# A decoder layer's opening in four contraction groups of four, the first begun tile by tile

## The chip, the cores and the metric

The kernel runs on one core of a Trainium2 chip. The metric is the device time of one execution in microseconds, the median of several runs. The engines are named as in the profile: PE (matrix products; PEld its weight loads), DVE (vector engine), ACT (scalar engine), POOL, and SP, whose queue issues nearly all transfers.

## The reference

One layer of a decoder, on 256 positions of width 2048, in float32. Only its beginning matters here:

```python
mod = jax.nn.silu(c) @ w_ada[l] + b_ada[l]               # c: (1, 2048), w_ada: (2048, 6 * 2048)
sh1, sc1, g1, sh2, sc2, g2 = jnp.split(mod[:, None, :], 6, axis=-1)
h = x * (1.0 + sc1) + sh1                                # x: (256, 2048)
proj = h @ w_in[l]                                       # then attention, DeltaNet, gates, LayerNorm
...
x = layer_norm(DEEPNORM_ALPHA * x + g1 * y, ln1_g[l], ln1_b[l])
h = x * (1.0 + sc2) + sh2
y = swiglu(h, w_ffn_in[l], w_ffn_out[l])
x = layer_norm(DEEPNORM_ALPHA * x + g2 * y, ln2_g[l], ln2_b[l])
```

So no product with `w_in` can start before `silu(c)` is there, columns of `w_ada` have been summed against it (shift and scale of the same rows of `h`), and x and `w_in` have been loaded.

## The kernel before

Everything is held transposed: `hTh`/`hTl` are h as 16 k tiles of 128 features x 256 positions. Every float32 operand of a product is split in two parts of the reduced type fp32r: `hi` is the value cast down (ACT, `split_w`, L221), `lo` what is missing (DVE, L222); for h that is done in `split` (L229, L230). A product of two such operands is three products: hi with the high part of h (L306), hi with its low part (L307), lo with the high part (L308), in `ws_mm`.

- **c.** `load_c` loads c into one row of `cb`, spreads it over 128 partitions by four products with a row of ones (`ps_c`, L136), and ACT writes silu of each quarter back to `cb` (L137).
- **Modulation.** `ada_opening` loads one column tile of `w_ada` after the other (1 MB each, L263) into a ring of four buffers (`r`, `ring`). `ada_sum` multiplies it by `cb` and sums, in one DVE instruction (L241), to one column of `adac`; the bias comes from `cols`. Column j is the shift of k tile j, column 16 + j its scale. `ada_to(n)` emits the sums up to the nth; `ada_goal` says how many are due at which step. The tiles of `w_ada` come in the order `ada_order`.
- **h.** `prep` forms h for some k tiles: scale plus one (`sc1p`, L442), scale and shift on ACT into `hf` (L445), then the split.
- **The opening's blocks.** `jobs` are 24 column blocks of `w_in`, 256 columns each: 16 for DeltaNet's q, k, v and 8 for attention's q, k. The contraction over 16 k tiles is cut in `GROUPS`, here 2, 3, 3, 4, 4 tiles. `startup(n)` passes over all 24 blocks for group n: load the block's k tiles of `w_in` (`raw`, `load_w`, L212), split, multiply. The first 19 blocks go to a PSUM buffer that is drained after each group: copied by ACT in the first group (L487), added by DVE to what is there in the others (L489). The last five (`KEPT`) stay in PSUM banks of their own (`mm_kept`) over all groups.
- **Order.** `step` and `do` write a program, `run(3)` starts loads and splits up to three steps ahead; the Tile layer then sets each engine's queue and the waits. A queue is served in order. The buffers are rings: six `raw`, four `hi`, four `lo`, four `r`.

Behind the opening stand `add_ba` (48 small products, L454), the two mixers, the projections and the feed-forward part, which the change does not touch.

Of the kernel before, what the change touches and what calls it, by code (L numbers as in the profile page):

```python
# [65 lines left out]
class Packed:  # L66
# [12 lines left out]

    def laid(self):  # L80
        out = np.empty(self.weight.size, np.float32)
        at = 0
        for k0, kn, c0, cn, by_column in self.tiles:
            n = P * kn * cn
# [9 lines left out]
def layer(ctx, tc, a, out):  # L94
# [32 lines left out]
    cb = perm.tile([P, D], F32, name="cb")  # L127

    def load_c():
        ones = e2("ones", [1, P])  # L130
        v_.memset(ones, 1.0)
        dma.dma_start(cb[0:1, :], a["c"])
        for i in range(4):
            ps = (pt.tile([P, 512], F32, tag="tp", name="ps_c") if i % 2 else
                  pg.tile([P, 512], F32, tag="gd", name="ps_c"))
            t_.matmul(ps, ones, cb[0:1, 512 * i:512 * i + 512], start=True, stop=True)  # L136
            s_.activation(cb[:, 512 * i:512 * i + 512], ps, AF.Silu)  # L137
# [12 lines left out]
    v_.memset(epsc[:, 0:1], RMS_EPS)  # L150
    v_.memset(epsc[:, 1:2], LN_EPS)
# [106 lines left out]
    def ada_opening(order, ahead, at_once, between):  # L258
        held, loaded = [], 0
        for n, col in enumerate(order):  # L260
            while loaded < min(at_once if n < at_once else n + ahead + 1, len(order)):
# [5 lines left out]
            ada_sum(col, 0, held.pop(0), 1)  # L267
# [9 lines left out]
    prog = []  # L277

# [95 lines left out]
    sc1p = perm.tile([P, KT], F32, name="sc1p")  # L374
# [40 lines left out]
    EARLY = 8  # L415

    def between(n):
        if n == 2 * GROUPS[0][1]:
            load_x(*GROUPS[0])

    ada1 = ada_opening(ada_order[:2 * KT + EARLY], 3, 2 * GROUPS[0][1], between)
# [7 lines left out]
    def ada_goal(n, i):  # L429
        ends = [2 * (k0 + kn) for k0, kn in GROUPS] + [2 * KT + EARLY]  # L430
        mark = 17
        if i >= mark:
            lo, hi, f = ends[min(n + 1, 5)], ends[min(n + 2, 5)], (i - mark) / len(jobs)
        else:
            lo, hi, f = ends[n], ends[n + 1], (i + len(jobs) - mark) / len(jobs) if n else (i + 1) / (mark + 1)
# [4 lines left out]
    def prep(k0, kn):  # L440
        q = slice(k0, k0 + kn)
        v_.tensor_scalar(sc1p[:, q], adac[:, 16 + k0:16 + k0 + kn], 1.0, None, op0=OP.add)  # L442
        for f in range(k0, k0 + kn):
            hf = e2("hf", [P, S])
            s_.activation(hf, x_sb[:, f, :], AF.Identity, bias=adac[:, f:f + 1], scale=sc1p[:, f:f + 1])  # L445
            split(hTh[:, f, :], hTl[:, f, :], hf)
# [10 lines left out]

    load_c()
    dma.dma_start(cols, a["cols"])
    ada_to(2 * GROUPS[0][1])  # L460
    prep(*GROUPS[0])

    KEPT = 5
    kept = []

    def startup(n):
        k0, kn = GROUPS[n]
        more = n + 1 < len(GROUPS)
        if more:
# [4 lines left out]
        for i, (c0, dst) in enumerate(jobs):  # L474
            def post(hi, lo, i=i, dst=dst):
# [4 lines left out]
                else:  # L480
                    if n == 0:
                        p, tag, b = ((pt, "tp", 2), (pt, "tp", 2), (pg, "gd", 2), (pg, "gd", 2), (pm, "mk", 1))[stays]
                        kept.append(p.tile([P, 512], F32, tag=tag, name="mm_kept", bufs=b))
                    ps = kept[stays]
                    ws_mm(ps, h_ops, hi, lo, k0, kn, n == 0, not more)
# [5 lines left out]
                if more and i == 17:  # L491
# [619 lines left out]
    jk = perm.tile([P, 40], F32, name="jk")  # L1111

# [271 lines left out]
```

## Time and profile before

| | |
|---|---|
| timed runs (us) | 1708.44, 1716.80, 1711.41; median 1711.41 |
| profiled execution, first to last instruction (us) | 1708.3 |
| mean granted TensorE clock | 0.992 |
| PE busy | 1651.7 us, 97% of the span, 11077 products |
| DVE, ACT busy | 1235.5 us (72%), 838.7 us (49%) |
| moved | 412.72 MB, mean 242 GB/s |

The page gives only the span for the profiled execution; what lies around it is not in the trace. "Idle before" in the tables is the time an engine sat idle ahead of such instructions, with the engine and line that ended most of it. A row of the timeline gives start, length, engine, line, operation, and in brackets the idle time before it and its releaser. In a row by stretches the columns are the stretch, its length, busy time of PE, PEld, DVE, ACT, POOL with counts of instructions, the granted TensorE clock, the share of the transfer engines, and GB/s.

### The profile page before, as it was taken

The numbers are of one execution on the slowest core, as the hardware profiler recorded it, in microseconds if no ns is written. First come the engines' busy times: TensorE is split into PE (matmuls) and PEld (weight loads), VectorE is DVE, ScalarE is ACT, GpSimd is POOL, SyncE is SP. The second block draws the span as 40 slices with busy tenths as digits, with TensorE's granted clock in tenths as the row PEclk, the third lists the DMA queues.
The fourth block names the chain that finished last, engine by engine and source line by source line (L and its number), as shares of the span: only waits on it lengthen the run. The fifth ranks groups of instructions, "written<-read, shape, count | busy, mean of one in ns | idle before, by whom it ended". The sixth has DMA issues, their size and how long they took to land.

```text
span 1708.3 us, 28200 instructions
## 1 busy us (share of the span) xinstructions
PE 1651.7 (97%) x11077; PEld 1482.3 (87%) x11077; DVE 1235.5 (72%) x1768; ACT 838.7 (49%) x1199; POOL 34.6 (2%) x60
## 2 busy tenths in 40 slices
PE   5899999999999998999999999999999999999997
PEld 4899999888999798889988998888888888888885
DVE  6899999787985676557989786666666666455454
ACT  3544445579653763364434454444444444433341
POOL 0000000010010000000000000000000000000000
PEclk9999999999999999999999999999999999999998
DMA  9999996666775577557899477777777776665661
GB/s 369 338 355 343 352 338 217 202 195 199 237 260 186 172 229 244 189 187 242 312 358 362 150 226 256 231 227 232 231 227 231 236 230 221 234 192 189 200 191 72
DMA packets 113750, 412.72 MB, mean 242 GB/s; under 512 B 13405, under 2 KB 14445, under 8 KB 108109
## 3 DMA queue, kind: packets, MB, share of 16 engines
q1 hardware_dynamic: 110178, 400.13, 69.4%
q0 software_dynamic: 3440, 10.80, 2.4%
q8 instruction: 87, 1.43, 0.3%
q14 instruction: 45, 0.37, 0.1%
HBM read 406.59 MB, written 4.28 MB: 241 GB/s over the span
## 4 chain that ended last, share of the span: by engine, by line
PE 61%; DVE 8%; DMA 5%; issue 2%; ACT 1%; DVEq 0%; ACTq 0%
PE mm L313 17%; PE mm L317 9%; PE mm L354 7%; PE mm L355 7%; PE mm L356 7%; DMA raw_a<-in_w_ada 4%; DVE lo L222 3%; PE mm L306 3%; PE mm L307 3%; PE mm L308 3%; DVE raw_a L241 1%; DMA Mb<-mbd 1%; PE ps L754 1%; DMA raw<-in_w_out 0%; ACT hi L221 0%
## 5 line engine op out<-in xcount | busy, mean ns | idle before, releaser
L221 ACT CAST hi<-raw 128x1024 fp32r<-128x1024 f32 (+2 forms) x576 | 582.6, 1015 | 706.2 <-PE mm L356 197.1
L222 DVE TENSOR_TENSOR lo<-raw,hi 128x1024 fp32r<-128x1024 f32 (+2 forms) x576 | 673.5, 1177 | 295.8 <-ACT hi L221 293.4
L306 PE MATMUL mm<-s,hi 128*128 128x256 f32 x1232 | 350.7, 285 | 15.9 <-ACT s L229 12.0
L308 PE MATMUL mm<-s,lo 128*128 128x256 f32 x1232 | 348.0, 283 | 13.1 <-DVE lo L222 12.9
L307 PE MATMUL mm<-s,hi 128*128 128x256 f32 x1232 | 346.8, 282 | 0.0
L313 PE MATMUL mm<-s,hi 128*128 128x512 f32 x1280 | 319.5, 392 | 0.0
L313 PEld LDWEIGHTS mm<-s,hi 128*128 128x128 f32 x1280 | 228.5, 188 | 39.4
L306 PEld LDWEIGHTS mm<-s,hi 128*128 128x128 f32 x1232 | 234.3, 190 | 21.0 <-ACT s L229 13.6
L308 PEld LDWEIGHTS mm<-s,lo 128*128 128x128 f32 x1232 | 235.8, 192 | 15.7 <-DVE lo L222 15.5
L307 PEld LDWEIGHTS mm<-s,hi 128*128 128x128 f32 x1232 | 234.8, 191 | 1.5 <-issue 1.1
L317 PEld LDWEIGHTS mm<-s,lo 128*128 128x128 f32 x1280 | 169.9, 188 | 13.6
L317 PE MATMUL mm<-s,lo 128*128 128x256 f32 x1280 | 171.9, 277 | 0.0
L354 PE MATMUL mm<-hi,ach 128*128 128x512 f32 x352 | 137.0, 389 | 0.0
L356 PE MATMUL mm<-hi,acl 128*128 128x512 f32 x352 | 136.9, 389 | 0.0
L355 PE MATMUL mm<-lo,ach 128*128 128x512 f32 x352 | 136.9, 389 | 0.0
L241 DVE CUSTOM_DVE_ANT_0 raw_a<-raw_a,cb,ada_half 128x1024 f32<-128x1024 f32 x56 | 71.7, 1280 | 53.3 <-DMA raw_a<-in_w_ada 53.3
L241 DVE CUSTOM_DVE_ANT_0 raw_a<-raw_a,cb,cols 128x1024 f32<-128x1024 f32 x56 | 71.8, 1281 | 51.1 <-DMA raw_a<-in_w_ada 51.0
L241 DVE CUSTOM_DVE_ANT_0 r<-r,cb,cols 128x2048 f32<-128x2048 f32 x40 | 93.4, 2346 | 9.4 <-ACT cb L137 9.4
L354 PE MATMUL mm<-hi,s 128*128 128x512 f32 x192 | 78.7, 410 | 0.0
L355 PEld LDWEIGHTS mm<-lo,ach 128*128 128x128 f32 x352 | 66.1, 188 | 13.8
L354 PEld LDWEIGHTS mm<-hi,ach 128*128 128x128 f32 x352 | 66.1, 188 | 13.8
L356 PEld LDWEIGHTS mm<-hi,acl 128*128 128x128 f32 x352 | 66.1, 188 | 13.6
(314 smaller groups left out, 2265.6 us busy)
## 6 DMA issues: line engine op xcount, KB each, us to landing
raw<-in_w_ffn_in SPq DMA_DIRECT2D x176, 512.0 KB, 4.3
raw<-in_w_in SPq DMA_DIRECT2D x160, 512.0 KB, 4.3
raw_a<-in_w_ada SPq DMA_DIRECT2D x112, 512.0 KB, 4.5
raw<-in_w_ffn_out SPq DMA_DIRECT2D x88, 512.0 KB, 4.2
r<-in_w_ada SPq DMA_DIRECT2D x40, 1024.0 KB, 8.0
raw<-in_w_in SPq DMA_DIRECT2D x48, 384.0 KB, 5.7
raw<-in_w_proj_gdn SPq DMA_DIRECT2D x32, 512.0 KB, 4.6
raw<-in_w_out SPq DMA_DIRECT2D x32, 512.0 KB, 5.9
```

The lines of the kernel that those rows point to most:

```text
L221: s_.copy(hi, raw)
L222: low = v_.tensor_tensor(lo, raw, hi.bitcast(F32), op=OP.subtract)
L241: v_.tensor_tensor_reduce(out=raw, in0=raw, in1=cb[:, n * part:n * part + n], scale=1.0, scalar=cols[:, col:col + 1] if first else h, op0= ...
L306: t_.matmul(o, hi[:, i, c], ah, start=(first and i == 0 and t == 0), stop=False)
L307: t_.matmul(o, hi[:, i, c], al, start=False, stop=False)
L308: t_.matmul(o, lo[:, i, c], ah, start=False, stop=(last and i == kn - 1 and t == 1))
L313: t_.matmul(box[t].rearrange("p (u i) -> p u i", u=2), hi[:, i, t * P:(t + 1) * P], both[k0 + i], start=(first and i == 0), stop=False)
L317: t_.matmul(box[t][:, :S], lo[:, i, t * P:(t + 1) * P], both[k0 + i][:, 0, :], start=False, stop=(last and i == kn - 1))
L354: t_.matmul(box[h], xh, hi[:, i, :], start=start, stop=False)
L355: t_.matmul(box[h], xh, lo[:, i, :], start=False, stop=False)
L356: t_.matmul(box[h], xl, hi[:, i, :], start=False, stop=stop)
L754: t_.matmul(ps[to, n, :], lhs(n), rhs(n), start=True, stop=True)
```

## The change

The opening has four groups of four k tiles. In the first, eight of the 24 blocks (`RAMP`: the last five, which stay in PSUM, and the first three) are begun tile by tile: for each of the k tiles 0 to 3 one x tile and two `raw` of four blocks x 256 columns of that one tile are loaded behind the tile's two columns of `w_ada`, and the products of four blocks run as soon as h of that tile is there (`ramp`). The other 16 blocks of the group follow as before, with four k tiles at once. Between the tiles of the ramp stand five products of zeros, ahead of c's products three, and behind them 22 (`warm`). The first `w_ada` column is summed in two halves. The table of ACT's functions is loaded by a small activation at the start. `prep` writes the high part of h straight from x, and a second activation the full value for the low part; the plus one of the scale goes into `cols`, once.

```diff
     def load_c():
         ones = e2("ones", [1, P])
         v_.memset(ones, 1.0)
         dma.dma_start(cb[0:1, :], a["c"])
+        ps = mm()
+        for i in range(3):
+            t_.matmul(ps, zero[:, :P], zero, start=True, stop=True)
...
     def ada_opening(order, ahead, between):
         held, loaded = [], 0
         for n, col in enumerate(order):
-            while loaded < min(at_once if n < at_once else n + ahead + 1, len(order)):
+            while loaded < min(n + ahead + 1, len(order)):
                 raw = ring[loaded % len(ring)]
                 dma.dma_start(raw, w_ada.tile(0, KT, order[loaded] * P, P, by_column=True))
                 held.append(raw)
                 loaded += 1
                 between(loaded)
-            ada_sum(col, 0, held.pop(0), 1)
+            raw = held.pop(0)
+            if n == 0:
+                for half in range(2):
+                    ada_sum(col, half, raw[:, 1024 * half:1024 * half + 1024], 2)
+            else:
+                ada_sum(col, 0, raw, 1)
             yield
...
+    def held_step(kept_raw, n, cn, post):
+        at = place["lo"]
+        prog.append((lambda: split_w(kept_raw(), n, cn, False, at), post, len(prog)))
...
-    GROUPS = [(0, 2), (2, 3), (5, 3), (8, 4), (12, 4)]
-    ada_order = [v * KT + j for k0, kn in GROUPS for j in range(k0, k0 + kn) for v in range(2)]
+    GROUPS = [(4 * n, 4) for n in range(4)]
+    ada_order = [v * KT + j for j in range(KT) for v in range(2)]
...
+    RAMP = [list(range(len(jobs) - KEPT, len(jobs) - 1)), [len(jobs) - 1, 0, 1, 2]]
+    raws = {}
 
     def between(n):
-        if n == 2 * GROUPS[0][1]:
-            load_x(*GROUPS[0])
+        if n % 2 or n > 2 * GROUPS[0][1]:
+            return
+        k = n // 2 - 1
+        load_x(k, 1)
+        for part, some in enumerate(RAMP):
+            raw = wp.tile([P, 1024], F32, tag="raw", name="raw", bufs=6)
+            dma.dma_start(raw, w_in.columns(k, [jobs[i][0] for i in some], 256))
+            raws[k, part] = raw.rearrange("p (k n) -> p k n", n=256)
...
+        if n == 0:
+            lo, hi, f = ends[0], ends[1], min((i - 2) / 14, 1)
...
     def prep(k0, kn):
-        q = slice(k0, k0 + kn)
-        v_.tensor_scalar(sc1p[:, q], adac[:, 16 + k0:16 + k0 + kn], 1.0, None, op0=OP.add)
         for f in range(k0, k0 + kn):
+            by = dict(bias=adac[:, f:f + 1], scale=adac[:, 16 + f:17 + f])
+            s_.activation(hTh[:, f, :], x_sb[:, f, :], AF.Identity, **by)
             hf = e2("hf", [P, S])
-            s_.activation(hf, x_sb[:, f, :], AF.Identity, bias=adac[:, f:f + 1], scale=sc1p[:, f:f + 1])
-            split(hTh[:, f, :], hTl[:, f, :], hf)
+            s_.activation(hf, x_sb[:, f, :], AF.Identity, **by)
+            v_.tensor_tensor(hTl[:, f, :], hf, hTh[:, f, :].bitcast(F32), op=OP.subtract)
...
+    zero = k1.tile([P, 512], F32R, tag="c2", name="zero", bufs=4)
+    v_.memset(zero.bitcast(F32), 0.0)
...
+    s_.activation(jk[:, 0:1], epsc[:, 0:1], AF.Silu)
     load_c()
     dma.dma_start(cols, a["cols"])
-    ada_to(2 * GROUPS[0][1])
-    prep(*GROUPS[0])
-
-    KEPT = 5
+    v_.tensor_scalar(cols[:, 16:32], cols[:, 16:32], 1.0, None, op0=OP.add)
+
+    def warm():
+        ps = mm()
+        two = [zero.rearrange("p (a b) -> p a b", b=b)[:, :, :b // 2] for b in (2, 32)]
+        for m in [zero] * 8 + [zero[:, 0:1].to_broadcast([P, 512])] * 3 + [zero[:, :S]] * 3 + two * 2 + [zero] * 4:
...
+            tc.keep_in_program_order(t_.matmul(o, zero[:, :P], m, start=True, stop=True))
+
+    def ramp(k, part):
+        def post(hi, lo):
+            some = RAMP[part]
...
+            for low in range(2):
+                for n, i in enumerate(some):
+                    for t in range(2):
+                        o, c = accs[i][:, t * S:(t + 1) * S], slice(t * P, (t + 1) * P)
+                        if low:
+                            last = k == 3 and t == 1 and i < len(jobs) - KEPT
+                            t_.matmul(o, lo[:, n, c], h_ops[0][k], start=False, stop=last)
+                        else:
+                            t_.matmul(o, hi[:, n, c], h_ops[0][k], start=(k == 0 and t == 0), stop=False)
+                            t_.matmul(o, hi[:, n, c], h_ops[1][k], start=False, stop=False)
+            if part and k < 3:
+                for _ in range(5):
+                    t_.matmul(kept[0], zero[:, :P], zero, start=False, stop=False)
+            if part and k == 3:
+                for i in some[1:]:
+                    s_.copy(jobs[i][1], pairs_of(accs[i]))
+
+        held_step(lambda: raws[k, part], 4, 256, post)
 
     def startup(n):
         k0, kn = GROUPS[n]
         more = n + 1 < len(GROUPS)
+        if n == 0:
+            for k in range(4):
+                do(lambda k=k: (ada_to(2 * k + 2), prep(k, 1)))
+                for part in range(2):
+                    ramp(k, part)
...
         for i, (c0, dst) in enumerate(jobs):
+            if n == 0 and i in RAMP[0] + RAMP[1]:
+                continue
```

What this makes of the queues, at three places. First SP, the issue of transfers from the program's start (`r` are columns of `w_ada`, 1 MB each; `raw` blocks of `w_in`). Before:

```order
L132 DMA cb<-in_c 1x2048
L459 DMA cols<-in_cols 128x256
L263 DMA r_95<-in_w_ada 128x2048 x2
L263 DMA r_96<-in_w_ada 128x2048
L263 DMA r_97<-in_w_ada 128x2048
L125 DMA x_sb<-in_xT 128x512
L212 DMA raw<-in_w_in 128x512 x4
L125 DMA x_sb<-in_xT 128x768
```

Now:

```order
L145 DMA cb<-in_c 1x2048
L497 DMA cols<-in_cols 128x256
L277 DMA r_93<-in_w_ada 128x2048 x2
L137 DMA x_sb<-in_xT 128x256
L449 DMA raw<-in_w_in 128x1024 x2
L277 DMA r_94<-in_w_ada 128x2048
L277 DMA r_95<-in_w_ada 128x2048
L137 DMA x_sb<-in_xT 128x256
L449 DMA raw<-in_w_in 128x1024 x2
```

The first `raw` have moved from behind four `w_ada` columns to behind two. Further on in SP's queue now, from the ramp's last tile (L449) to the blocks that are loaded as before (L226):

```order
L137 DMA x_sb<-in_xT 128x256
L449 DMA raw<-in_w_in 128x1024 x2
L277 DMA r_93<-in_w_ada 128x2048 x2
L277 DMA r_94<-in_w_ada 128x2048
L226 DMA raw<-in_w_in 128x1024 x4
L137 DMA x_sb<-in_xT 128x1024
```

Three columns of `w_ada` stand between the ramp's last `raw` and the next block's. The same place in DVE's queue now: the ramp's last `lo`, then the sums, then the `lo` of the next blocks (`s_86` is the low part of h).

```order
L236 TENSOR_TENSOR lo<-raw,hi 128x1024
L479 TENSOR_TENSOR s_86<-hf,s_85 128x256
L236 TENSOR_TENSOR lo<-raw,hi 128x1024
L255 ISA r_93,adac<-r_93,cb,cols 128x2048
L255 ISA adac 128x1
L255 ISA r_93,adac<-r_93,cb,cols 128x2048
L255 ISA adac 128x1
L255 ISA r_94,adac<-r_94,cb,cols 128x2048
L255 ISA adac 128x1
L236 TENSOR_TENSOR lo<-raw,hi 128x1024 x4
```

Three sums stand ahead of the four `lo` that the next blocks need. Last PE, from its start to the first real products; before:

```order
L136 MATMUL ps_c<-cb,ones 128x512 x4
L306 MATMUL mm<-s_86,hi 128x256 x2
L307 MATMUL mm<-s_87,hi 128x256
L308 MATMUL mm<-s_86,lo 128x256
L306 MATMUL mm<-s_86,hi 128x256
```

Now (`s_85` and `s_86` are the high and low part of h):

```order
L148 MATMUL mm<-zero 128x512 x3
L152 MATMUL ps_c<-cb,ones 128x512 x4
L508 MATMUL mm<-zero 128x512 x11
L508 MATMUL mm<-zero 128x256 x7
L508 MATMUL mm<-zero 128x512 x4
L534 MATMUL mm_kept<-s_85,hi 128x256 x4
L535 MATMUL mm_kept<-s_86,hi 128x256
```

25 products of zeros stand ahead of the first real one, on both sides of c's. Behind the products of `ba` all queues hold the same instructions in the same order as before.

More of the change, by code (lines that the diff above doesn't have):

```diff
@@ L78, in tile, with columns @@
         return src
+    def columns(self, k, starts, cn):
+        n = len(starts) * cn
+        src = bass.AP(tensor=self.ap.tensor, offset=self.ap.offset + self.at, ap=[[n, P], [1, n]])
+        self.tiles.append((k, 1, starts, cn, False))
+        self.at += P * n
+        return src
     def laid(self):
@@ L83, in laid @@
         for k0, kn, c0, cn, by_column in self.tiles:
+            if isinstance(c0, list):
+                block = np.concatenate([self.weight[k0 * P:(k0 + 1) * P, c:c + cn] for c in c0], axis=1)
+                out[at:at + block.size] = block.reshape(-1)
+                at += block.size
+                continue
             n = P * kn * cn
@@ L127, in layer @@
     cb = perm.tile([P, D], F32, name="cb")
+    jk = perm.tile([P, 40], F32, name="jk")
     def load_c():
@@ L256, in ada_sums, with ada_opening @@
                 yield 1.35
-    def ada_opening(order, ahead, at_once, between):
+    def ada_opening(order, ahead, between):
         held, loaded = [], 0
         for n, col in enumerate(order):
-            while loaded < min(at_once if n < at_once else n + ahead + 1, len(order)):
+            while loaded < min(n + ahead + 1, len(order)):
                 raw = ring[loaded % len(ring)]
@@ L373, in layer @@
     h_ops = [[t[:, k, :] for k in range(KT)] for t in (hTh, hTl)]
-    sc1p = perm.tile([P, KT], F32, name="sc1p")
     def g8(slot, nm, shape, dt=F32):
@@ new lines, in layer @@
+    warm()
+    kept = []
+    accs = {}
+    def ramp(k, part):
+        def post(hi, lo):
+            some = RAMP[part]
+            if k == 0:
+                for i in some:
+                    stays = i - len(jobs) + KEPT
+                    if stays < 0:
+                        accs[i] = mm()
+                        continue
+                    p, tag, b = ((pt, "tp", 2), (pt, "tp", 2), (pg, "gd", 2), (pg, "gd", 2), (pm, "mk", 1))[stays]
+                    accs[i] = p.tile([P, 512], F32, tag=tag, name="mm_kept", bufs=b)
+                    kept.append(accs[i])
+            for low in range(2):
[15 more added lines that the diff above has]
+        held_step(lambda: raws[k, part], 4, 256, post)
@@ L480, in post @@
                 else:
-                    if n == 0:
-                        p, tag, b = ((pt, "tp", 2), (pt, "tp", 2), (pg, "gd", 2), (pg, "gd", 2), (pm, "mk", 1))[stays]
-                        kept.append(p.tile([P, 512], F32, tag=tag, name="mm_kept", bufs=b))
                     ps = kept[stays]
-                    ws_mm(ps, h_ops, hi, lo, k0, kn, n == 0, not more)
+                    ws_mm(ps, h_ops, hi, lo, k0, kn, False, not more)
                 if n == 0 if stays < 0 else not more:
@@ L490, in post @@
                 ada_to(ada_goal(n, i))
-                if more and i == 17:
+                if more and i == (17 if n else 16):
                     prep(*GROUPS[n + 1])
```

19 lines of the change are left out of this document (12 added, 7 removed).

## The prediction, made before the changed kernel was run

> **What bounds the kernel now.** I read the page first, then PE's waits, then the opening in order of time.
>
> ```profile
> span 1708.3 us, 28200 instructions
> PE   5899999999999998999999999999999999999997
> DMA  9999996666775577557899477777777776665661
> ```
>
> PE is full but for the first slices (42.7 us each), and DMA is full there: the kernel is bound by PE's work, and idle PE time in the opening is what can be won. PE's waits in the first 400 us (us in total, times, longest):
>
> ```profile
> PE mm L306 <- ACT s L229: 12.0, 1, 12.0
> PE mm L306 <- ACT hi L221: 3.9, 5, 2.0
> PE mm L308 <- DVE lo L222: 3.5, 4, 1.4
> PE ps_c L136 <- DMA cb<-in_c: 2.6, 1, 2.6
> ```
>
> The opening is 24 column blocks x 16 k tiles x 6 = 2304 products of 256 columns. Behind the last of them stand the products of `ba`; and in its dense part PE never waits:
>
> ```profile
> L454 PE MATMUL ps_ba<-s,wbh x32: 276/276/279, 309.3 to 314.5; 128*32 128x256 f32 x32
> ...
> 170.00:300.00 130.00, 130.00 (x1106) 130.00 (x1105) 122.39 (x153) 61.55 (x75) 2.57 (x4) 1.00 0.85 302
> ```
>
> 1106 products in 130 us are 0.1175 us each, so 2304 are 270.7 us. The opening ends at 309.2 (just ahead of 309.3): 309.2 - 270.7 = **38.5 us lost before**. Where they lie, in order of time (start, length, engine):
>
> ```profile
> 2.62 7.16 PE L136 MATMUL ps_c<-cb,ones 1*128 1x512 f32 x8 [2.62 <-DMA cb<-in_c]
> 4.69 0.60 ACT L137 ACTIVATE cb<-ps_c 128x512 f32<-128x512 f32 x1 [0.86 <-PE ps_c L136]
> 9.58 0.33 SPq L212 DMA_DIRECT2D raw<-in_w_in  x1
> 10.44 2.35 DVE L241 CUSTOM_DVE_ANT_0 r<-r,cb,cols 128x2048 f32<-128x2048 f32 x1 [9.40 <-ACT cb L137]
> 12.03 0.33 SPq L125 DMA_DIRECT2D x_sb<-in_xT  x1
> 18.39 1.96 ACT L221 CAST hi<-raw 128x512 fp32r<-128x512 f32 x3 [7.98 <-DMA raw<-in_w_in]
> 21.78 0.80 PE L306 MATMUL mm<-s,hi 128*128 128x256 f32 x2 [12.00 <-ACT s L229]
> 25.18 0.34 PE L306 MATMUL mm<-s,hi 128*128 128x256 f32 x1
> 31.84 0.28 PE L308 MATMUL mm<-s,lo 128*128 128x256 f32 x1
> ...
> 34.15 0.38 PE L306 MATMUL mm<-s,hi 128*128 128x256 f32 x1 [2.04 <-ACT hi L221]
> 36.48 0.58 PE L308 MATMUL mm<-s,lo 128*128 128x256 f32 x1 [1.17 <-DVE lo L222]
> 41.98 0.41 PE L308 MATMUL mm<-s,lo 128*128 128x256 f32 x1
> 42.19 0.37 PE L306 MATMUL mm<-s,hi 128*128 128x256 f32 x1
> ```
>
> The first real product starts at 21.78, PE runs dry at 32 and again until 36.48, and from then to 42.19 products stand 0.21 us apart instead of 0.1175 (41.98 to 42.19). The rest is small waits up to 170. The granted clock (second last but two of the columns) says what the slow stretch is, and the same rows say what the transfers do (last column, GB/s):
>
> ```profile
> 0.00:10.00 10.00, 7.16 (x8) 2.49 (x8) 0.24 (x3) 3.26 (x5) 0.89 (x5) 1.00 0.71 233
> 10.00:20.00 10.00, 0.00 (x0) 0.00 (x0) 9.56 (x9) 1.91 (x4) 0.00 (x0) 1.00 1.03 410
> 20.00:30.00 10.00, 8.22 (x56) 8.22 (x57) 7.52 (x12) 5.94 (x12) 0.00 (x0) 1.00 1.02 420
> 30.00:40.00 10.00, 6.64 (x38) 6.03 (x38) 9.89 (x11) 3.61 (x6) 0.00 (x0) 0.78 1.03 405
> ...
> 50.00:60.00 10.00, 8.49 (x66) 7.68 (x65) 8.33 (x12) 8.72 (x18) 0.00 (x0) 1.00 0.79 264
> ...
> 36.00:37.00 1.00, 0.52 (x2) 0.53 (x3) 1.00 (x3) 0.00 (x0) 0.00 (x0) 0.50 1.04 395
> ```
>
> So the opening's start is bound by bytes: 2.33 MB have come by 10 us, 6.43 by 20, 10.63 by 30, 14.68 by 40, then 0.405 MB per us. A load is usable some 1.9 us after its last byte by this count: the first `raw` is byte 4.98 MB of the queue (0.27 of small loads, four `w_ada` columns of 1.049, 0.26 of x, 0.26 itself), which is 16.5 us, and the cast that waited for it began at 18.39; the second `w_ada` column (2.37 MB, 10.1 us) released SP at 12.03.
>
> **The change, costed.** One k tile of the new ramp loads two `w_ada` columns, one x tile and two `raw` of 0.524 MB: 3.28 MB, 8.0 us. The engines need less for it:
>
> ```profile
> L222 DVE TENSOR_TENSOR lo<-raw,hi 128x1024 fp32r<-128x1024 f32 x48 | 58.0, 1219 | 3.2 <-ACT hi L221 2.9
> L241 DVE CUSTOM_DVE_ANT_0 r<-r,cb,cols 128x2048 f32<-128x2048 f32 x12 | 28.1, 2345 | 0.0
> L221 ACT CAST hi<-raw 128x1024 fp32r<-128x1024 f32 x47 | 49.0, 1049 | 57.3 <-PE mm L307 44.0 <-PE mm_kept L307 9.2 <-ACT cv L578 2.0
> ...
> L489 DVE TENSOR_TENSOR kq<-kq,mm 128x512 f32<-128x512 f32 x16 | 10.9, 682 | 3.6 <-PE mm L308 3.5
> ...
> L445 ACT ACTIVATE hf<-x_sb,adac,sc1p 128x256 f32<-128x256 f32 x16 | 9.1, 598 | 24.1 <-DVE sc1p L442 13.7 <-DVE s L230 10.4
> L230 DVE TENSOR_TENSOR s<-hf,s 128x256 fp32r<-128x256 f32 x16 | 6.1, 419 | 0.3 <-ACT s L229 0.3
> ```
>
> DVE: 2 x 2.35 + 2 x 1.22 + 0.42 = 7.6 us. PE: 48 x 0.1175 = 5.6 us. Transfers set the pace.
> - *Tile 0.* Its first `raw` is byte 3.02 MB, 11.7 us, usable at 13.6; cast 1.05; the new `prep` writes h itself 0.6 later: first product at 15.2 against 21.78. The two `w_ada` sums are done by then (the second column lands at 12.0, plus 2.35).
> - *Tile 3.* 24 us later: first product about 39.3, last about 45.
> - *The hole.* On SP three more `w_ada` columns stand ahead of the next `raw` (the order shown above). Bytes: 0.27 + 4 x 3.28 + 3 x 1.049 + 0.524 = 17.05 MB, 45.8 us, usable 47.7, cast done 48.8. On DVE the three sums stand ahead of `lo` as well: third column usable 46.4, summed 48.8, `lo` 50.0. So PE is dry from 45 to **50**, with 192 products behind it (two more go at 48.8, worth 0.2).
> - *Half clock.* The gap of 31.9 to 36.5 with four products in it brought 0.50 until 42.19; this one is alike, and no zero products stand in it (they follow tiles 0 to 2 only). Released 3.4 us after a start (21.78 to 25.18) or 5.7 (36.48 to 42.19); half of that is lost: 1.7 to 2.9. Bounds: 0 (the clock stays up) to 3.4 (twice 3.4 at half speed). I take 2.4, as the row of 36.48 is the nearest.
> - *Rest of group 0:* 16 blocks of 24 products, 2.82 us each; they need 0.524 MB plus about half a `w_ada` column, 1.12 MB or 2.77 us. The transfers are just ahead; DVE needs 1.22 + 1.2 = 2.4 us per block. In ACT's queue a cast stands behind a copy of the block two earlier: copy 0.6, cast 1.05, `lo` 1.22 make 2.9 against 2.82 to hide it. Bounds 0 and the 3.9 us that five such waits for `hi` cost before; I take 0.8, nearer to zero because the miss is 0.1 a block.
> - *Groups 1 to 3* are dense: a block gives DVE 1.22 + 0.68 + 8/24 x 2.35 = 2.7 us in 2.82. The 19 additions that a fifth group needed (19 x 0.68 = 13 us) go from DVE, and 16 activations replace 16 shorter casts on ACT, which is half idle: both beside PE's work, credited nothing; lost cover would cost under 1 us.
> - *Products of zeros:* 22 behind c's products. At the slow spacing they end at 9.8 + 15 x 0.43 + 7 x 0.21 = 17.7, 2.5 us behind tile 0's data; each tile leaves 8.0 - 5.6 = 2.4 us, less 1.1 for its five zero products, so this is caught up by tile 2 and costs nothing while the hole is there. The zero memset and the three zero products before c go while c is on its way (2.62).
> - *Table load, memsets, `cols` plus one, first `w_ada` column in halves:* the ACT row at 4.69 waits for PE, not for the table; the DVE start moves from 10.44 to about 9.6 (SP's issue at 9.58, the eighth after the column, tells its landing). All of it lies ahead of bytes that come at 13.6: nothing.
>
> Sum: opening's end = 50.0 - 0.2 + 2112 x 0.1175 (248.2) + 2.4 + 0.8 = 301.2, against 309.2: **8.0 us gained**. Behind the `ba` products the queues hold the same instructions in the same order, so all of it should reach the end. The profiled execution spans 1708.3 and the timed median is 1711.4, 3.1 more; I carry the difference over: 1711.4 - 8.0 = **1703.4 us**.
>
> [...]
>
> **Rivals.**
> - *The clock stays up, or the hole is short.* [...] Then 2.4 + 0.8 come back: 11.2 gained, 1700.2. Against it: the transfers ahead of the next `raw` are fixed by the order.
> - *Transfers bind the rest of group 0.* From the first `raw` behind the hole to the last of the group come 15 more `raw`, four x tiles and six columns: 7.9 + 0.5 + 6.3 = 14.7 MB. At 0.405 that is 36 us against PE's 45; at the 264 GB/s of 50 to 60 it is 55.5: 47.7 + 55.5 + 1.05 + 1.2 + 2.8 = 108.3 for the group's end against 98.1. At 0.30 in between, 3.5 us are lost: 4.5 gained, 1706.9. Against it: in those rows SP waited for buffers, so the rate is not the limit.
> - *Slower: products of zeros do not raise or hold the clock.* Place: the ramp. At 0.21 per product and 0.43 per zero product a tile takes 48 x 0.21 + 5 x 0.43 = 12.2 us instead of the 8.0 of its bytes; from 17.7 on the ramp ends at 17.7 + 4 x 12.2 - 2.1 = 64.4 instead of the hole's 50: 14.4 lost, 6.4 slower, 1717.8, and more if the clock is late after it. It decides once half clock lasts through three tiles (17.7 + 3 x 12.2 + 5.6 = 59.9, against 50.0 plus the 8.0 gained). Against it: the real products alone released the clock within 3.4 us at 21.78.
>
> **How the numbers follow.** A measurement of this kernel tells about 0.5% (8.6 us) from no change; the forecast of 8.0 is just below it. The main case, 6 to 10 us gained (1701.4 to 1705.4), has 0.50; 0.2 of it is beyond 8.6. The first rival 0.22, all beyond. The second 0.18, all within. The third 0.07, and 0.03 for what I don't see, shared between no change and slower. So faster 0.2 + 0.22, rounded to 0.43; slower 0.07; same 0.50. The range reaches into the second rival's far half and past the first: 1698 to 1710.5, leaving out the third.
>
> **What would show it.** Right: first ramp product near 15.2; tiles 8.0 us apart; PE dry from 45 to 50 with `lo` or `hi` as releaser; clock 0.50 right behind it; `ba` near 301. Wrong: DMA under 400 GB/s between 10 and 80 us, a ramp at half clock, or waits of PE in groups 1 to 3 above 2 us.

## The result, and the profile after

The changed kernel is slower: 1727.88 us (median of 4 runs, 1727.55 to 1732.76) against 1711.81 (1708.44 to 1716.80), a ratio of 1.0091 with a 95% interval of [1.0067, 1.0115]. 8.0 us were to be gained; 16 were lost.

The page of the changed kernel (the forty slices are 43.3 us here):

```profile
span 1731.0 us, 28124 instructions
PE   9999999999899998999999999999999999999997
DMA  9989886576685577557999468777777776766662
```

The first slice of PE went from 5 to 9, and the opening did begin earlier. PE's waits in the first 400 us of the changed kernel (us in total, times, longest):

```profile
PE mm L331 <- DVE lo L236: 4.0, 6, 1.7
PE mm L329 <- ACT hi L235: 2.4, 1, 2.4
PE mm L148 <- DVE epsc L493: 1.5, 1, 1.5
```

The four rows of before made 22.0 us; these three make 7.9. The wait of 12.0 for the first h is gone. Four landmarks say where the rest of the span went: the first product of `ba` (end of the opening), the first and last product of the feed-forward part's first projection (the wide products, L313 before), and the span's end. Before, the line of the wide products (least, median and greatest duration in ns, then first and last start):

```profile
L313 PE MATMUL mm<-s,hi x1280: 388/392/398, 1012.6 to 1450.9; 128*128 128x512 f32 x183
```

The same two groups in the changed kernel, by tile and by line:

```profile
L487 PE MATMUL ps_ba<-s,wbh x32: 276/280/283, 305.4 to 310.8; 128*32 128x256 f32 x32
```
```profile
L336 PE MATMUL mm<-s,hi x1280: 391/394/398, 1026.1 to 1473.0; 128*128 128x512 f32 x183
```

| stretch (us) | before | changed | difference |
|---|---|---|---|
| start to first `ba` product | 309.3 | 305.4 | -3.9 |
| `ba` to first wide product | 703.3 | 720.7 | +17.4 |
| first to last wide product | 438.3 | 446.9 | +8.6 |
| last wide product to the end | 257.4 | 258.0 | +0.6 |
| span | 1708.3 | 1731.0 | +22.7 |

The 22.7 us are 6.6 more than the 16.1 between the medians: the changed kernel's profile is that of the slowest of its four runs (1732.76, the next 1728.17), at a mean granted clock of 0.989 against 0.992 in the profile of before. The table shows where time went in these two executions, and not what each stage costs on the median. Still, the loss lies in stages whose code and whose order of instructions the change leaves alone. In the wide stretch PE is never idle in either kernel, at full clock, and gets through fewer products. The same two stretches of time, in the dense opening and in the wide products, before and changed (columns as in the prediction's rows):

```profile
1050.00:1400.00 350.00, 350.00 (x2043) 307.84 (x2042) 226.21 (x273) 169.35 (x223) 0.00 (x0) 1.00 0.72 230
```
```profile
170.00:300.00 130.00, 130.00 (x1098) 130.00 (x1097) 121.33 (x154) 61.21 (x76) 3.11 (x5) 1.00 0.82 284
1050.00:1400.00 350.00, 350.00 (x2002) 304.75 (x2001) 224.84 (x272) 165.63 (x219) 0.00 (x0) 1.00 0.73 227
```

2043 products in 350 us became 2002: 0.1713 us each became 0.1748. In the opening 1106 became 1098. PE is "busy" all the time; its count says that it is slower.

What differs for these products is where their operands lie. The change drops the small tile `sc1p` (64 bytes a partition) and allocates `jk` (160 bytes) near the start instead of late. So everything between moves: h, which is also the memory of the feed-forward part's moving operand, lies 160 bytes further up, and all that is allocated behind `sc1p` and `jk` (`raw`, `hi`, `lo`, the small buffers) 64 bytes further down. Byte addresses within a partition (the distance between h and the weights follows from the order and the sizes of the tiles in the two kernels):

| | before | changed |
|---|---|---|
| high and low part of h (`s0`, `s1`) | 31872, 48512 | 32032, 48672 |
| first `raw`, `hi`, `lo` | 66240, 90816, 107200 | 66176, 90752, 107136 |

All k tiles, blocks, halves and ring buffers of these operands are multiples of 256 bytes apart. So one number describes a kernel: the distance from h to the weights, modulo 256. Before it is 90816 - 31872 = 58944, which leaves 64; changed, 96. It is a label of the buffers, though, and not the distance of every pair of operands: in all kernels alike, the wide products take their moving operand from 128 bytes into h's memory (`aT(tag, 32)`) and their `lo` weights from 128 bytes into a `lo` buffer (`place["lo"] = 32`). At the label 64 the opening's weights lie 64 bytes from their operand, `hi` and `lo` alike; in the wide products `lo` lies 64 and `hi` 192 from it.

### The profile page after: what moved, and what is told of

The parts are those of the page before. It is cut to its first block, busy times and chain, and to the rows that moved or that the text cites. A ratio compares the mean times of both kernels' runs of the same rounds, so it can differ in the third digit from the quotient of the medians.

```text
span 1731.0 us, 28124 instructions
## 1 busy us (share of the span) xinstructions
PE 1686.1 (97%) x11117; PEld 1509.6 (87%) x11117; DVE 1225.2 (71%) x1724; ACT 835.8 (48%) x1176; POOL 34.5 (2%) x60
## 4 chain that ended last, share of the span: by engine, by line
PE 78%; DVE 9%; DMA 7%; issue 3%; ACT 2%; SPq 0%; POOL 0%; DVEq 0%; ACTq 0%; POOLq 0%
PE mm L336 17%; PE mm L340 9%; PE mm L377 8%; PE mm L379 8%; PE mm L378 8%; PE mm L331 7%; PE mm L329 7%; PE mm L330 7%; DVE lo L236 4%; DMA raw_a<-in_w_ada 3%; DMA raw<-in_w_in 1%; DVE r L255 1%; DMA Mb<-mbd 1%; PE mm_kept L331 1%; PE mm_kept L329 1%
## 5 line engine op out<-in xcount | busy, mean ns | idle before, releaser
L235 ACT CAST hi<-raw 128x1024 fp32r<-128x1024 f32 x552 | 577.2, 1049 | 710.5 <-PE mm L379 199.4
L236 DVE TENSOR_TENSOR lo<-raw,hi 128x1024 fp32r<-128x1024 f32 x552 | 672.1, 1223 | 318.1 <-ACT hi L235 315.4
L329 PE MATMUL mm<-s,hi 128*128 128x256 f32 x1208 | 345.2, 286 | 2.4 <-ACT hi L235 2.4
L330 PE MATMUL mm<-s,hi 128*128 128x256 f32 x1208 | 342.0, 283 | 0.0
L336 PE MATMUL mm<-s,hi 128*128 128x512 f32 x1280 | 323.7, 395 | 0.0
L336 PEld LDWEIGHTS mm<-s,hi 128*128 128x128 f32 x1280 | 229.1, 188 | 43.2
L329 PEld LDWEIGHTS mm<-s,hi 128*128 128x128 f32 x1208 | 230.0, 191 | 4.8 <-ACT hi L235 2.6
L330 PEld LDWEIGHTS mm<-s,hi 128*128 128x128 f32 x1208 | 230.1, 190 | 1.6 <-issue 1.1
L255 DVE CUSTOM_DVE_ANT_0 r<-r,cb,cols 128x2048 f32<-128x2048 f32 (+1 forms) x40 | 92.5, 2321 | 4.1 <-ACT cb L153 4.1
```

The costliest lines, as they stand in the source:

```text
L235: s_.copy(hi, raw)
L236: low = v_.tensor_tensor(lo, raw, hi.bitcast(F32), op=OP.subtract)
L255: v_.tensor_tensor_reduce(out=raw, in0=raw, in1=cb[:, n * part:n * part + n], scale=1.0, scalar=cols[:, col:col + 1] if first else h, op0= ...
L329: t_.matmul(o, hi[:, i, c], ah, start=(first and i == 0 and t == 0), stop=False)
L330: t_.matmul(o, hi[:, i, c], al, start=False, stop=False)
L336: t_.matmul(box[t].rearrange("p (u i) -> p u i", u=2), hi[:, i, t * P:(t + 1) * P], both[k0 + i], start=(first and i == 0), stop=False)
```

## The experiments

Theory: the changed kernel loses by its addresses, and its new order gains about what was forecast. Rival: the new order itself disturbs the later stages.

**The new order at the old addresses.** `sc1p` stays, unused but as the target of the small activation that loads the table, and `jk` is allocated where it was:

```diff
-    jk = perm.tile([P, 40], F32, name="jk")
...
+    sc1p = perm.tile([P, KT], F32, name="sc1p")
...
-    s_.activation(jk[:, 0:1], epsc[:, 0:1], AF.Silu)
+    s_.activation(sc1p[:, 0:1], epsc[:, 0:1], AF.Silu)
...
+    jk = perm.tile([P, 40], F32, name="jk")
```

> The changed kernel with every tile of the long-lived pools back at the SBUF address it had before (the dropped 64-byte sc1p is kept as a dummy, the 160-byte jk is allocated late again); every queue holds the same instructions in the same order as in the changed kernel. Theory A (the loss behind the opening is a slower spacing of the products that comes from shifted addresses: h 160 bytes up, raw, hi, lo and all behind 64 bytes down): the wide products of the feed-forward input go back from 0.2325 us to 0.227 us apart, the 9 us of drift between 1000 and 1450 us and most of that between 450 and 680 vanish, and the opening's 4 us or a little more stay: 1705 to 1713 us. Rival B (the loss comes from the changed order or from where the clock windows fall, not from addresses): the spacing and the time stay, 1724 to 1732 us.

Measured: 1709.40 us against 1716.33 of the kernel before on that chip, ratio 0.9963 [0.9944, 0.9981]. The order of every queue is that of the changed kernel. The wide products are back:

```profile
1050.00:1400.00 350.00, 350.00 (x2042) 307.84 (x2041) 228.34 (x276) 169.49 (x224) 0.00 (x0) 1.00 0.73 231
```

**The old order at the new addresses.**

```diff
+    jk = perm.tile([P, 40], F32, name="jk")
...
-    sc1p = perm.tile([P, KT], F32, name="sc1p")
...
+    sc1p = pad[:, :KT]
...
-    jk = perm.tile([P, 40], F32, name="jk")
```

> The kernel before, with the same instructions in the same order, and only the addresses of the changed kernel: jk allocated early (h and everything up to it 160 bytes up), sc1p taken out of its pool (raw, hi, lo and everything behind 64 bytes down). Theory A: slower by what the addresses cost, 12 to 24 us, 1723 to 1736 us, with the wide products 0.2325 us apart. Rival B: no change, 1708 to 1716 us.

Measured: 1730.83, ratio 1.0100 [1.0076, 1.0125], with none of the change in it. 1994 wide products in the 350 us:

```profile
1050.00:1400.00 350.00, 350.00 (x1994) 304.70 (x1993) 221.02 (x267) 164.63 (x218) 0.00 (x0) 1.00 0.72 225
```

The two together settle the sign: the addresses cost 1.0% under the old order and 1.3% under the new one (1.0091 / 0.9963); the new order is worth -0.37% at the old addresses and -0.1% at the new ones, which its intervals don't tell from -0.37%.

**Half of the shift each.** First `jk` alone moved to the front (h up by 160), then `sc1p` alone left out (weights down by 64).

> The kernel before with only one half of the shift: jk allocated early, so the two tiles of h (and the small ones ahead of them) lie 160 bytes higher, all else as before. Theory A, if it is the distance between the moving operand h and the weights hi and lo that counts: some of the loss in the opening, and the feed-forward part, whose moving operand lies in another place, slower only if its operand is one of these two tiles; 1712 to 1730 us. Rival B: 1708 to 1716 us.

> The kernel before with only the other half of the shift: sc1p out of its pool, so raw, hi, lo and all behind them lie 64 bytes lower, h as before. Theory A: the weights move against the moving operand and against each other's place in memory not at all; slower where the moving operand stays, 1712 to 1735 us, and with the run before it the two halves say which of the operands it is. Rival B: 1708 to 1716 us.

Measured: 1740.87, ratio 1.0150 [1.0126, 1.0174], and 1734.03, 1.0119 [1.0093, 1.0145]. Neither half is quick, so it is not that one of the two alone had a good place and lost it. What is left is the place of one relative to the other, or each one's own place.

**Distance or place.** One kernel moves weights and h together by 64 bytes (distance as before, another place); one moves the weights by 128 alone (as before if the distance counted modulo 128):

```diff
+    gap = perm.tile([P, 16], F32, name="gap")
...
-    pad = k1.tile([P, 48], F32, name="pad")
+    pad = k1.tile([P, 32], F32, name="pad")
```
```diff
-    sc1p = perm.tile([P, KT], F32, name="sc1p")
+    sc1p = perm.tile([P, KT + 32], F32, name="sc1p")
...
-    pad = k1.tile([P, 48], F32, name="pad")
+    pad = k1.tile([P, 16], F32, name="pad")
```

> The kernel before, with h and the weights both 64 bytes further up: their distance is that of before, the place of each modulo 128 bytes is not. Theory of the distance: as before, ratio 0.997 to 1.003, wide products 0.171 us apart. Rival (where h or the weights begin within 128 bytes counts, not their distance): ratio 1.008 to 1.015, wide products 0.175 us.

> The kernel before, with raw, hi, lo and all buffers behind them 128 bytes further up; h and everything ahead of it stays; queues and order are those of before. Theory (only the distance of the weights from the moving h, modulo 128 bytes, counts; it stays 64): as before, ratio 0.997 to 1.003, wide products of the feed-forward part 0.171 us apart on the mean. Rival (the distance modulo 256 or more, or the place of the weights itself counts): ratio 1.008 to 1.015 and wide products 0.175 to 0.176 us, as in the three shifted kernels so far.

Measured: both together 1713.45 against 1713.00, ratio 0.9991 [0.9973, 1.0010]; weights alone by 128, 1730.15, 1.0094 [1.0063, 1.0124]. It is the distance, and for the kernel as a whole its period is not 128 bytes: that guess of mine fell. The loss of this second kernel lies behind the opening, however: its products from 170 to 300 keep the pace of before, 1107 for 1106, and its `ba` starts at 307.5 for 309.3.

**The period, and other distances.** The purest control allocates one scratch tile of 256 bytes behind h instead of ahead of it, so that h alone moves, by 256:

```diff
-    ada_half = perm.tile([P, 64], F32, name="ada_half")
...
+    ada_half = perm.tile([P, 64], F32, name="ada_half")
     sc1p = perm.tile([P, KT], F32, name="sc1p")
```

> The kernel before, with only the two buffers of h (which the feed-forward part uses for its moving operand too) 256 bytes further down; the weights and all else but one small scratch tile stay. So far the distance from the moving operand to the weights, modulo 256 bytes, was 64 in the two quick kernels and 0, 96, 160 and 192 in the four slow ones. Theory (the distance modulo 256 counts; it stays 64): ratio 0.997 to 1.003, wide products 0.171 us apart, 1106 to 1149 products in 170 to 300. Rival (a longer period): ratio 1.008 to 1.015, wide products 0.175.

Two more try the distances 128 (`sc1p` longer by 64 bytes) and 32 (a gap of 32 bytes ahead of h, `jk` shorter by as much).

> The kernel before, with the weights 64 bytes further up, so a distance of 128 modulo 256. Theory (64 is a good distance and the others are not): slower, ratio 1.005 to 1.015, wide products 0.174 to 0.176. Rival (one distance only is bad in each stage and 128 is as good or better): ratio 0.994 to 1.002, with 0.113 us from product to product all through the opening.

> The kernel before, with h 32 bytes further up and the weights where they were: a distance of 32 modulo 256. Theory (64 is a good distance, half of it is not): ratio 1.004 to 1.015, wide products 0.173 to 0.176. Rival (a window of at least 32 bytes around 64 is good): ratio 0.997 to 1.003, 0.171.

Measured: h moved by 256, 1715.47 against 1715.46, ratio 0.9997 [0.9975, 1.0019]; distance 128, 1729.82, 1.0092 [1.0060, 1.0124]; distance 32, 1733.91, 1.0106 [1.0075, 1.0137]. The rows of these three in that order:

```profile
1050.00:1400.00 350.00, 350.00 (x2042) 307.82 (x2041) 226.85 (x275) 169.91 (x224) 0.00 (x0) 1.00 0.73 230
```
```profile
1050.00:1400.00 350.00, 350.00 (x1997) 307.53 (x1997) 224.31 (x272) 165.53 (x220) 0.00 (x0) 1.00 0.72 227
```
```profile
1050.00:1400.00 350.00, 350.00 (x1989) 304.49 (x1989) 222.14 (x268) 164.18 (x218) 0.00 (x0) 1.00 0.72 225
```

The kernels so far in one table (products in 1050 to 1400, then the landmarks' stretches in us, from one profile each):

| distance mod 256 | kernel | ratio | wide products | first to last wide | `ba` to wide |
|---|---|---|---|---|---|
| 64 | before | 1 | 2043 | 438.3 | 703.3 |
| 64 | old order, h and weights +64 | 0.9991 | 2042 | 438.3 | 703.2 |
| 64 | old order, h -256 | 0.9997 | 2042 | 438.3 | 710.1 |
| 64 | new order, old addresses | 0.9963 | 2042 | 438.3 | 714.2 |
| 0 | old order, weights -64 | 1.0119 | 2002 | 446.8 | 717.0 |
| 32 | old order, h +32 | 1.0106 | 1989 | 450.0 | 716.0 |
| 96 | old order, new addresses | 1.0100 | 1994 | 448.9 | 711.3 |
| 96 | changed kernel | 1.0091 | 2002 | 446.9 | 720.7 |
| 128 | old order, weights +64 | 1.0092 | 1997 | 447.9 | 716.5 |
| 160 | old order, h +160 | 1.0150 | 1983 | 451.1 | 720.3 |
| 192 | old order, weights +128 | 1.0094 | 2000 | 447.3 | 712.6 |

Every kernel at 64 is quick and every other one is 0.9 to 1.5% slower. The wide stretch takes 438.3 us at 64, to a tenth, and 446.8 to 451.1 elsewhere. That the period is 256 bytes rests on one kernel, the one with h moved by 256.

**The hole.** Next the change's own mechanism, at old addresses. The columns of `w_ada` behind the eighth are issued only once the ramp is summed, so that the next `raw` follow the ramp's directly:

```diff
-            while loaded < min(n + ahead + 1, len(order)):
+            while loaded < min(n + ahead + 1, 8 if n < 8 else len(order)):
```

> The changed kernel with the addresses of before, and with the columns of w_ada behind the eighth issued only when the ramp's four tiles are summed, so that the next raw blocks follow the ramp's own in SP's queue instead of three columns. Theory (the hole of 45 to 50 us and the half clock behind it are due to these three columns): PE is busy through 45 to 50, no half clock there, the ba products begin 5 to 7 us earlier than in the changed kernel with old addresses (about 298), ratio 0.992 to 0.994 against before. Rival (the bytes only come later: the columns are missing at the step from group 0 to group 1): what is won at 45 to 50 is lost at 85 to 105, ba again at 303 to 305, ratio 0.996 to 0.998.

Measured: 1704.50 against 1713.00, ratio 0.9948 [0.9928, 0.9968]. The new order at old addresses, and then this kernel:

```profile
45.00:50.00 5.00, 1.09 (x4) 0.89 (x5) 5.00 (x6) 4.29 (x7) 0.00 (x0) 0.87 1.03 410
50.00:55.00 5.00, 5.00 (x25) 5.00 (x25) 2.76 (x3) 1.40 (x3) 0.00 (x0) 0.50 1.02 415
55.00:60.00 5.00, 5.00 (x43) 5.00 (x43) 3.37 (x3) 2.62 (x5) 0.00 (x0) 0.94 1.02 415
60.00:65.00 5.00, 5.00 (x47) 5.00 (x46) 3.08 (x5) 3.94 (x6) 0.00 (x0) 1.00 1.03 422
```
```profile
45.00:50.00 5.00, 4.81 (x42) 4.82 (x43) 1.43 (x2) 3.59 (x6) 0.00 (x0) 1.00 1.02 426
50.00:55.00 5.00, 5.00 (x47) 5.00 (x46) 5.00 (x4) 1.17 (x2) 0.00 (x0) 1.00 1.00 415
55.00:60.00 5.00, 4.07 (x36) 3.87 (x35) 4.84 (x6) 2.47 (x5) 0.00 (x0) 1.00 1.02 413
60.00:65.00 5.00, 3.55 (x28) 3.35 (x29) 4.49 (x6) 2.91 (x5) 0.00 (x0) 1.00 1.02 418
```

The hole and the half clock are gone: 42 and 47 products where 4 and 25 ran. Some of it is given back 10 us later (36 and 28 for 43 and 47): PE waits there for `hi` (1.6 us) and `lo` (0.8), and four sums of the columns that now come later take up DVE between 50.94 and 60.68. The theory holds in its mechanism, with a ratio just short of the expected 0.992 to 0.994; the rival's loss does come, but it is smaller than the gain and comes at 55 to 65 instead of 85 to 105: of the 60 products won in the first two rows 26 are lost again in the last two. The first `ba` product starts at 294.8 instead of 304.2, but part of that is another spacing in this profile (see the last section), which is not the hole's.

**Two columns ahead instead of three while group 0 lasts**, on top of this:

```diff
-            while loaded < min(n + ahead + 1, 8 if n < 8 else len(order)):
+            while loaded < min(n + ahead + (n not in range(8, 16)), 8 if n < 8 else len(order)):
```

> The changed kernel with the addresses of before and the late columns of the run before this (columns of w_ada behind the eighth only when the ramp is summed), now two columns ahead instead of three while group 0 lasts. Theory (behind the ramp PE waits because three columns come at once and later ones of group 2 take bytes from group 0): first ba product at 291 to 295 (294.7 with three), PE 1 to 2 us busier in 55 to 65; ratio 0.991 to 0.995. Rival (fewer columns ahead make DVE wait for them, with lo queued behind): ba at 296 or later, ratio 0.995 to 0.998.

Measured: 1712.19 against 1715.46, ratio 0.9986 [0.9964, 1.0008], `ba` at 299.3. 55 to 65 is better, as expected, by 0.4 and 1.2 us, but PE then waits once for 4.0 us for `lo`, until 115.85:

```profile
PE mm L330 <- DVE lo L235: 8.1, 7, 4.0
```

That `lo` starts on DVE at 114.58, right behind a column's sum (from 112.31); in the run before, the `lo` at this place stands ahead of the next sum. DVE waits for no column there, so this is the order of its queue and not missing bytes. The rival came nearer, with `ba` late and `lo` queued behind a sum, though not for its reason. The kernel with three columns ahead is the best of this study; against the new order at old addresses (0.9963) its interval does not set it apart.

**Without products of zeros**, the new order at old addresses:

```diff
-        ps = mm()
-        for i in range(3):
-            t_.matmul(ps, zero[:, :P], zero, start=True, stop=True)
...
-    warm()
...
-            if part and k < 3:
-                for _ in range(5):
-                    t_.matmul(kept[0], zero[:, :P], zero, start=False, stop=False)
```

> The changed kernel with the addresses of before and without its products of zeros: the three ahead of c, the 22 behind, and five behind each of three tiles are left out; the rest is as it was. Theory (the ramp waits for bytes, and the hole at 45 to 50 takes up what is lost ahead of it): first real product near 15.3 instead of 18, half clock for the first 3 to 7 us of the ramp, ba products within 1.5 us of the changed kernel with old addresses (304.2), ratio 0.995 to 0.998. Rival (the clock has to be raised ahead of the ramp): the ramp runs at half clock into the third tile, 4 to 7 us later at ba, ratio 0.999 to 1.001.

Measured: 1710.34 against 1713.00, ratio 0.9987 [0.9966, 1.0007]; its interval overlaps that with zeros. The profile tells more than the total. First real products in the changed kernel, and then without zeros:

```profile
10.15 7.17 PE L508 MATMUL mm<-zero 128*128 128x512 f32 x22
17.16 0.63 PE L534 MATMUL mm_kept<-s,hi 128*128 128x256 f32 x4
```
```profile
14.73 1.22 PE L530 MATMUL mm_kept<-s,hi 128*128 128x256 f32 x4 [4.92 <-ACT s L473]
18.41 1.38 PE L528 MATMUL mm_kept<-s,lo 128*128 128x256 f32 x8
19.62 0.28 PE L530 MATMUL mm_kept<-s,hi 128*128 128x256 f32 x1
```

With zeros the first four products stand 0.12 us apart ((0.63 - 0.28) / 3), without them more than 0.2 until some 19 us: with products of zeros ahead the quick spacing is there from the start. The granted clock reads 1.00 from 15 to 20 us in both, so it is the spacing that shows it. Without them the ramp starts 2.4 us sooner, and the granted clock falls once more at 39.5 (0.71 from 40 to 45). But the step from group 0 to group 1 shows the same dip at the same time in both, first with zeros and then without:

```profile
100.00:105.00 5.00, 3.32 (x29) 3.12 (x28) 4.09 (x4) 2.92 (x5) 0.00 (x0) 1.00 0.80 301
```
```profile
100.00:105.00 5.00, 3.31 (x28) 3.22 (x28) 4.32 (x5) 2.89 (x6) 0.00 (x0) 1.00 0.61 202
```

Through the opening's first 100 us the zeros are worth nothing, as the theory had it: by then 598 real products have started with them and 602 without. Its `ba` even starts at 297.7 instead of 304.2, but by another spacing in this profile (last section), not for want of zeros. So `ba` was not within the expected 1.5 us, and the ratio of 0.9987 lies just above the expected 0.995 to 0.998. The rival's ramp at half clock into the third tile did not come either: the products stand 0.11 to 0.12 us apart from 19.62 on, still in the first tile. Whether the zeros are worth something on the total, the two intervals leave open.

## Why the prediction was wrong

Its own steps, in order:

- *First ramp product at 15.2.* Measured 17.16, because the 22 zero products stand ahead of it; the data were ready near 14.73, as the kernel without zeros shows. The prediction had the zeros end at 17.7 and be caught up, and so it was.
- *Ramp paced by bytes, tile 3 from 39.3, last product about 45.* Measured 38.76, the last one ending at 45.1, with 405 to 421 GB/s from 10 to 45. Right.
- *PE dry from 45 to 50 by three columns ahead of the next `raw`.* Right to 0.6 us (45.1 to 49.4), releasers included:

```profile
44.27 0.86 PE L532 MATMUL mm<-s,lo 128*128 128x256 f32 x6
47.53 0.39 PE L329 MATMUL mm<-s,hi 128*128 128x256 f32 x1 [2.39 <-ACT hi L235]
47.75 0.28 PE L330 MATMUL mm<-s,hi 128*128 128x256 f32 x1
49.40 0.53 PE L331 MATMUL mm<-s,lo 128*128 128x256 f32 x1 [1.37 <-DVE lo L236]
```

- *Half clock, 2.4 us lost.* It lasted from 49.5 to 52.9, 3.4 us at a granted clock of 0.50, of which half is lost: 1.7, the lower end of the step. The same order at old addresses had half clock from 48.7 to 55.6 (0.87, 0.50 and 0.94 in the three rows from 45 to 60) and lost 3.4, so the size is not fixed by the order.

```profile
50.00:53.00 3.00, 3.00 (x16) 3.00 (x16) 2.75 (x3) 1.10 (x2) 0.00 (x0) 0.52 1.03 419
```

- *Rest of group 0, 0.8 us lost.* Counted by products, the group ended at 96.6 instead of 98.1: 1.5 better than forecast.
- *Groups 1 to 3 dense.* Wrong: the 1728 products behind group 0 took 208.7 us (96.6 to 305.3) instead of 203.0. At the step from group 0 to group 1 PE runs 3.32 of 5 us, where the kernel before had no gap; with the row ahead of it 2.0 us are idle. It is not the second rival (transfers bind), although the step lies where transfers are busy: PE waits for `lo`, and on DVE that `lo` stands behind a column's sum and behind an addition that itself waits for PE. No transfer ends a wait of an engine between 94 and 106. The prediction counted DVE's work per block (2.7 us of 2.82) and not the order in which it comes. The kernel before at 100 to 105, the two rows of the changed kernel, and its waits:

```profile
100.00:105.00 5.00, 5.00 (x45) 5.00 (x44) 5.00 (x8) 3.10 (x5) 0.00 (x0) 1.00 0.95 324
```
```profile
95.00:100.00 5.00, 4.73 (x40) 4.53 (x40) 4.60 (x5) 3.69 (x5) 0.00 (x0) 1.00 1.01 370
100.00:105.00 5.00, 3.32 (x29) 3.12 (x28) 4.09 (x4) 2.88 (x6) 0.00 (x0) 1.00 0.77 292
```
```profile
97.25 2.35 DVE L255 CUSTOM_DVE_ANT_0 r<-r,cb,cols 128x2048 f32<-128x2048 f32 x1
100.28 0.69 DVE L573 TENSOR_TENSOR kq<-kq,mm 128x512 f32<-128x512 f32 x1 [0.68 <-PE mm L331]
100.89 3.49 DVE L236 TENSOR_TENSOR lo<-raw,hi 128x1024 fp32r<-128x1024 f32 x3
102.16 0.38 PE L331 MATMUL mm<-s,lo 128*128 128x256 f32 x1 [1.68 <-DVE lo L236]
```

- *Opening's end at 301.2.* Measured 305.3. The slower spacing (1098 products for 1106 in 130 us) is another 1.5 us over 1728 products; with the dip that is 3.5 of the 5.7 lost behind group 0, and 2.2 I could not place. The old order at these addresses ran 1110 products in the same 130 us, so this spacing is not the addresses' doing alone.
- *"Behind the `ba` products the queues hold the same instructions in the same order, so all of it should reach the end."* **This is the step that failed.** Its first half is true. The second assumed that the same instructions in the same order take the same time; they lie at other addresses, and PE ran them 2% slower in the wide stretch (446.9 us for 438.3). The old order at the new addresses alone took 1.0100 times as long. With the addresses put back the change is worth 0.37% [0.19, 0.56], 6.4 us on that chip's 1716.33, beside 8.0 forecast. So the forecast of the new order was near, and the forecast of the kernel was wrong. The nearness is in part luck: the interval is 3.3 to 9.6 us, and in that kernel's profile `ba` comes 5.1 us earlier than before (304.2 for 309.3), not 8.0, because groups 1 to 3 were not dense.
- *The slower rival*, products of zeros not raising or holding the clock, did not happen: behind them the first real products stood 0.12 us apart. The kernel is slower for a reason that was on no list.

The diff showed it: a tile `sc1p` that no longer exists and a `jk` that is used at the start. I costed the instructions that these two lines add and remove, and never asked what moves behind them.

What stays open: of the 17.4 us between `ba` and the wide products, the kernel with old order and new addresses has 8.0 (711.3 for 703.3). The new order at old addresses has 10.9, which no slower spacing explains. Part of it is half clock: the changed kernel has 23.9 us at a granted clock of 0.50 there, before 6.8; for the new order at old addresses its mean clock of 0.989 gives 17 to 18 by my estimate (0.011 of 1714.7 us is what 37.7 at half clock lose; 6.9 of them lie in the opening, and at the span's end the other two profiles have 13.9 and 12.3). Compared product by product, 6.5 of the 17.4 us arise at one place, around a stretch of the changed kernel at half clock (0.50 from 438.6 to 445.4). The mean clock differs between executions of one and the same kernel: 27 runs of the kernel before on one chip had mean clocks of 0.986 to 0.993 and took 1707.92 to 1722.56 us. The control that moved h by 256 bytes, with the old order and a ratio of 0.9997, has 17.0 us at 0.50 or 0.51 there and takes 6.8 us more. And the profile of the new order at old addresses is that of the slowest of its ten runs (1716.49, median 1709.40). On the same chip the mean clock of these ten is 0.9896, that of 13 runs of before 0.9905; by my estimate that is 1.5 us (0.0009 of 1716), the time that the added half clock costs if PE sets the pace throughout. Whether the new order costs something behind `ba` beyond that, one profile of each can't say.

## What to carry to other kernels

Dropping a tile of 64 bytes and allocating one of 160 early moved the buffers behind them by as much, and on this kernel such moves alone cost 0.9 to 1.5% wherever they changed the distance from h to the weights modulo 256, more than the edit was worth. When stages that an edit does not touch change their pace, compare the number of products in a stretch where PE is full, then the addresses, before looking for a cause in the order. Before comparing two profiles stage by stage, look where each stands among the timed runs of its kernel. To judge an edit of the order, run it with the old addresses; and keep a tile whose size nobody needs if its bytes hold the others in place.

## What the runs showed of the hardware

- **Product spacing went with where weights and moving operand lie to each other.** At a granted clock of 1.00, without a wait, 256 columns in the opening took 0.113 or 0.118 us from product to product at a distance of 64 bytes modulo 256 (1149 products in 130 us with the late columns, 1106 before), and 0.117 to 0.120 at the six other distances tried (from 854 products in the 100 us from 200 to 300, in the old order at 96, down to 835 at 160). In the opening 192 was as good as before (1107 and 1106 products in 130 us); in the wide stretch, where the products with `hi` lie 128 bytes off the label, 64 alone was quick, with 438.3 us against 446.8 to 451.1. Why PE's pace hangs on these addresses the rows do not show: whether the reads of weights and of moving operand hinder each other, or another engine's access hinders one of them, was not told apart. The buffers of weights moved together with all those behind them. h moved with only small tiles beside it, by 32 and by 160 bytes, and both kernels were slow (1.0106, 1.0150); moved almost alone by 256 it was neutral.
- **Two spacings at the same addresses.** At a distance of 64 the opening ran at 0.118 in some stretches and at 0.113 in others, and stayed in one for 100 us and more. 170 to 300 in the new order at old addresses, and then with the late columns:

```profile
170.00:300.00 130.00, 130.00 (x1106) 130.00 (x1106) 121.10 (x154) 61.92 (x78) 3.11 (x5) 1.00 0.82 284
```
```profile
170.00:300.00 130.00, 130.00 (x1149) 129.75 (x1149) 124.07 (x164) 64.76 (x81) 3.11 (x5) 1.00 0.81 283
```

  43 products more in 130 us, at equal clock and equal transfers: 5 us, which is half of the 9.4 between their `ba` products (294.8 and 304.2). The kernel before has both, 0.113 from 140.1 to 145.8 and 0.118 from 146.6 to 152.7. From 170 to 300 the three kernels at this distance in the old order ran 1106, 1106 and 1107 products, so it may go with the order; what chooses the spacing is open. It is as large as most edits of this opening.
- **Half clock comes in windows of 3.4 us, at another phase in each profile.** Ahead of the one at the span's end, the profile of before has a granted clock of 0.50 in two stretches of 6.83 us, from 35.54 and from 684.08; the changed kernel's has it for 3.41 us from 49.49 and 902.82 and for 6.83 from 438.61, 691.20 and 704.85. In each of the two profiles these starts lie whole multiples of 3.413 us apart (648.54 is 190 of them), and counted from the span's start those of one profile do not lie so to those of the other (49.49 less 35.54 is 4.09 of them). The same stage in the kernel before and in the one with h moved by 256 bytes, first at full and then at half clock:

```profile
627.50:630.90 3.40, 3.40 (x33) 3.40 (x32) 3.37 (x7) 1.06 (x1) 0.00 (x0) 1.00 0.76 223
```
```profile
627.50:630.90 3.40, 3.40 (x18) 3.40 (x17) 3.30 (x9) 0.79 (x1) 0.00 (x0) 0.51 0.83 260
```

  33 products and 18, in kernels whose ratio is 0.9997. So a few microseconds in one profile's middle stages are not yet a cost of the edit.
- **Behind products of zeros the first real ones ran at the quick spacing.** With 22 of them ahead, in 7.17 us, the first real products stood 0.12 us apart from 17.16 on; without them 0.21 apart, as at half clock, for some 4 us (14.73 to 19.0).
